# Filter work of the first pair in two tails, norm factors one token tile later, four gates ahead of the last branch

## The chip, the cores and the metric

The kernel runs on one core of a Trainium2 chip. The metric is the device time of one execution in microseconds (us); a comparison goes by the median of several executions.

## The reference

The input `x` has 512 tokens of width 1024, all float32. Two blocks of two layers each follow one another: two layers of the first kind (layer a), then two pairs of the second kind (layer b, cross attention, MLP).

```
def first_block(x, ...):                       # layer a, l = 0, 1
    h = rms_norm(x, norm_g[l]);  p = h @ w_in[l]
    y_a = short_conv_mixer(...); y_b = sparse_attention_mixer(...); y_c = pool_mixer(...)
    g = sigmoid(mgate)
    x = x + (g[0] * y_a + g[1] * y_b + g[2] * y_c) @ w_o[l]
...
def second_block(h, mem, ...):                 # pair i = 0, 1
    (aq, ak, av, hy, gq, gk, gv, go, glr, gates) = split_cols(rmsnorm(h) @ w_in[i])
    y_a = attention_mixer(aq, ak, av, ...) @ w_br_attn[i]
    spec = hyena_filter_spectra(z_pos, window, hy_w1[i], ...)   # depends on weights alone
    y_b = hyena_mixer(hy, hy_conv[i], spec, hy_skip[i]) @ w_br_hyena[i]
    y_c = gla_mixer(...) @ w_br_gla[i]
    h = h + (gate[0] * y_a + gate[1] * y_b + gate[2] * y_c) @ w_out[i]
    h = h + memory_cross_attention(...)
    h = h + square(relu(rmsnorm(h) @ mlp_w1[i])) @ mlp_w2[i]
```

In both attentions the heads of queries and keys are normalised: each head of 64 is multiplied by the reciprocal root of its mean square, and rotated by its position. `hyena_filter_spectra` sends a table of positions through a small network of two sine layers, forms four filters (two orders, two directions) under a window, and takes their Fourier transform.

## The kernel before, in words

Every float32 product is made of three matmuls of a rounded type, a high and a low part of each operand (`mm3`, lines 242 to 244). So each weight tile is loaded by an SP DMA into `wr`, its high part `wh` is made on ACT (line 220) and its low part `wl` on DVE (line 221), and the same split makes the high and low parts of every activation (`big`). `gemm_t` and `gemm_wide` are the two loops over such products: `gemm_t` makes 256 output columns at a time (a column chunk: 48 matmuls for 1024 rows of weights, 24 for 512), with the result transposed; `gemm_wide` makes 512 columns for four tiles of 128 tokens, each in a PSUM tile of its own, and then calls `evac(t, ps[t])` for the four tiles in turn.

The order of instructions on each engine is fixed when the program is built, from the order of the code and from priorities (`high_priority`); at run time each engine goes through its own list and waits where an operand is not there.

**Norm factors.** Queries and keys come out of `gemm_wide`. Its `evac` (`ev_qk`, lines 707 to 724 in layer a; `heads`, from line 1315, in layer b) copies the PSUM tile to SBUF on ACT (`lift`, line 326, a buffer of the pool s2), sums squares on DVE (`sums64`, line 578), and calls `rsqrt_small`: one small DVE instruction (line 583), then a power on POOL (line 584) over 4 to 8 columns, in the tile `sgk`. The next DVE instruction of that tile is the one that reads POOL's result (line 719 to `sig` in layer a, line 1327 in layer b); the rotation (lines 534 to 537) and the splits stand around it.

**Filters of a pair.** `filters(l)` sets up a generator, and `step_background` takes one step of it after every column chunk of `gemm_t`. For pair 0 that happens in the tail of the second layer a (26 chunks), for pair 1 in the first MLP (31 chunks). The steps are, in order: two sine layers (a matmul at line 1067, a chain of seven DVE instructions at lines 1069 to 1074, a sine on ACT at line 1075), the features `hA`, `hB` (lines 1081 to 1083), and then for each order `od` four steps that multiply features with taps (lines 1097, 1098) and with a window tile `win` that POOL's DMA queue loads into one buffer (line 1100), the sum of magnitudes (line 1108) that the matmul at line 1130 adds up, and eight transform steps.

**The last branch of layer b.** `finish_merge` calls `gate_out`, which for each pair of output tiles makes two gates (a column chunk of 48 matmuls on `h`), and multiplies them with a chunk of 24 matmuls on the branch's output `yb` (weights `w_br_hyena`). With `lead` 2 the gates of the first pair are made ahead. `yb` is what the second long convolution leaves: its last matmuls (`sd<-df,hy`), eight DVE instructions (lines 1290 to 1293), a product with `x2` from DRAM (line 1477) and a split.

Of the kernel before, what the change touches and what calls it, by code (L numbers as in the profile page):

```python
# [10 lines left out]
F32 = mybir.dt.float32  # L11
F32R = mybir.dt.float32r
# [7 lines left out]
P = 128  # L20
# [111 lines left out]
class Kernel:  # L132
    def __init__(self, ctx, tc, A, out, scratch=None):
        self.ctx, self.tc, self.A, self.out = ctx, tc, A, out
        self.nc = tc.nc
        pool = lambda name, **kw: ctx.enter_context(tc.tile_pool(name=name, **kw))
        self.cst = pool("cst", bufs=1)
        self.wp = pool("wp", bufs=3)
        self.bp = pool("bp", bufs=10)
        self.xp = pool("xp", bufs=9)  # L140
        self.sp = pool("sp", bufs=6)
        self.pp = pool("pp", bufs=6)
        self.dp = pool("dp", bufs=1, space=DRAM)
# [4 lines left out]
        self.background = None  # L148
        self.consts()

# [493 lines left out]
    def layer_a(self, l, st, next_norm, side=None):  # L644
# [62 lines left out]
        def qkv(c):  # L707
# [5 lines left out]
            def ev_qk(t, ps):  # L713
# [292 lines left out]

    def filters(self, l):

        nc, A = self.nc, self.A
        spec = self.dp.tile([2, 4, 3, P, 512], F32, tag=f"spec{l}", name=self.nm("spec"), bufs=1)  # L1010
        self.background, self.halves = self.filter_steps(l, spec), False
        next(self.background)
        return spec

    def filter_steps(self, l, spec):
        with self.tc.tile_pool(name=f"fg{l}", bufs=1, reuse_waits="tile") as fp:
            self.hp = fp
            yield from self.filter_body(l, spec, fp)

    def filter_body(self, l, spec, fp):  # L1020
# [3 lines left out]
        w12 = fp.tile([P, P], F32, tag="w12", name=self.nm("w12"))  # L1024
        cols = self.small(8, "hycol", bufs=1)
        nc.gpsimd.dma_start(w12[:33, 0:64], A["hy_w1_2"][l])
        nc.gpsimd.dma_start(w12[:64, 64:128], A["hy_w2_2"][l])
        for i, a in enumerate((A["hy_b1_2"][l], A["hy_b2_2"][l], A["hy_freq_2"][l, 0], A["hy_freq_2"][l, 1])):
            nc.gpsimd.dma_start(cols[:64, i : i + 1], a.rearrange("(p o) -> p o", o=1))
        zp = own("win")  # L1030
        nc.gpsimd.dma_start(zp[:33], A["c_zpos"])
        h1 = self.p2()
        h2 = self.p2()

# [28 lines left out]

        nxt = taps_w(0)
        for dst, lhs, rhs, i in ((h1, w12[:33, 0:64], zp[:33], 0), (h2, w12[:64, 64:128], h1[:64], 1)):
            ps = self.ps_sd()
            nc.tensor.matmul(ps[:64], lhs, rhs, start=True, stop=True)
            arg, n = self.p2()[:64], self.p2()[:64]
            nc.vector.tensor_scalar(arg, ps[:64], cols[:64, i : i + 1], cols[:64, 2 + i : 3 + i], ALU.add, ALU.mult)
            nc.vector.tensor_scalar(n, arg, 1.0 / (2 * math.pi), 12582912.0, ALU.mult, ALU.add)  # L1070
            nc.vector.tensor_scalar(n, n, 12582912.0, None, ALU.subtract)
            for part in (6.28125, 0.0019350051879882812, 3.0199159819567e-07):
                nc.vector.scalar_tensor_tensor(arg, n, -part, arg, ALU.mult, ALU.add)
            nc.vector.tensor_scalar(arg, arg, 3.1415925, -3.1415925, ALU.min, ALU.max)
            nc.scalar.activation(dst[:64], arg, AF.Sin)
            yield
        hB_ = hB.bitcast(F32)
        nc.gpsimd.memset(hB_[64:P], 0.0)
        nc.gpsimd.memset(hB_[64:65], 1.0)
        nc.gpsimd.memset(hB_[96:97], 1.0)  # L1080
        nc.vector.tensor_copy(hB[:64], h2[:64])
        nc.scalar.copy(hA[:64], h2[:64])
        nc.vector.tensor_tensor(hA[64:P], h2[:64], hA[:64].bitcast(F32), ALU.subtract)
        yield
        e = fp.tile([P, 4, 512], F32, tag="fe", name=self.nm("fe"))
        o = fp.tile([P, 4, 512], F32, tag="fo", name=self.nm("fo"))
        for od in range(2):
            w3 = nxt
# [45 lines left out]
            for m, (b, i) in enumerate(steps):  # L1134
# [19 lines left out]
                nc.gpsimd.dma_start(spec[od, b, i], f)  # L1154
                if m == 6 and od == 0:
                    nxt = taps_w(1)
# [138 lines left out]
    def layer_b(self, l, st, spec, next_norm):  # L1295
# [22 lines left out]
        def heads(c, t, ps, ng):  # L1318
# [6 lines left out]
            self.rsqrt_small(ss, ss, 1.0 / 64, n)  # L1325
            rs = rstd[:, t : t + 1]
            nc.vector.tensor_scalar(sigs[c][:, t * 4 : t * 4 + 4], ss[:, :4], rs, 0.125, ALU.mult, ALU.mult)
            v = lambda x: x.rearrange("p (g h d) -> p g h d", g=ng, h=2)
# [3 lines left out]
            self.split(qhl[c][:, t, :, 0], qhl[c][:, t, :, 1], r[:, :4])  # L1332
            if n > 4:
                nc.vector.tensor_scalar(ss[:, 4:6], ss[:, 4:6], rs, None, ALU.mult)
                nc.vector.tensor_tensor(r[:, 4:6], r[:, 4:6], ss[:, 4:6].unsqueeze(2).to_broadcast([P, 2, 64]), ALU.mult)
                self.split(kv[:, t, 0:2, 0], kv[:, t, 0:2, 1], r[:, 4:6])

        def ev_qkv(t, ps):
            ps = self.lift(ps)
            vs = ps[:, 384:512].rearrange("p (h d) -> p h d", h=2)  # L1340
            heads(0, t, ps, 3)
            self.split(kv[:, t, 2:4, 0], kv[:, t, 2:4, 1], vs, scale=rstd[:, t : t + 1])

        gv = self.big(F32)
# [3 lines left out]
        def ev_qg(t, ps):  # L1348
            nc.scalar.activation(gv[:, t, 0:256], ps[:, 256:512], AF.Copy, scale=rstd[:, t : t + 1])
            heads(1, t, self.lift(ps[:, 0:256]), 2)  # L1350

# [94 lines left out]
        with self.tc.tile_pool(name=f"gb{l}", bufs=16, reuse_waits="tile") as self.gp:  # L1446
            turn_lr()
            b, on = self.gla_begin(l, glr)
            self.gemm_t(W, 2304, 512, KD, h, ev_qk)
            self.background, self.halves = self.gla_steps(l, b, on, qk, gv), True  # L1450
            self.gate_out(W, 3872, h, A["w_br_attn_2"][l], ya, M, True, None)
# [12 lines left out]
        with self.tc.tile_pool(name=f"hb{l}", bufs=8, reuse_waits="tile") as self.hp:  # L1464
# [9 lines left out]
            for c in range(4):  # L1474
# [359 lines left out]
    def run(self, stop=None):  # L1834
# [3 lines left out]

        def fill(l):
            spec[l] = self.filters(l)  # L1840

# [49 lines left out]
```

## Time and profile before

| | |
|---|---|
| median of 3 runs | 3386.12 us (3383.73 to 3386.2) |
| profiled execution | 3385.05 us, span 3382.9 us |
| granted TensorE clock, mean | 0.997 |
| PE busy | 3309.0 us |
| DVE busy | 2335.5 us |
| ACT busy | 1509.5 us |
| POOL busy | 308.0 us |

Busy time is that in which the engine has an instruction under way. Matmuls overlap, so PE is counted busy while it works at any rate; how densely they follow is read from their starts or from their number in a window.

### The profile page before, as it was taken

How to read it: one execution, taken by the hardware profiler on the slowest of the kernel's cores; microseconds unless marked ns; L12 is line 12 of the kernel's file. 1: busy time of each engine (PE TensorE's matmuls, PEld its weight loads, DVE VectorE, ACT ScalarE, POOL GpSimd, SP SyncE). 2: the span in 40 equal slices, each digit the busy share in tenths (PEclk: the TensorE clock that was granted, in tenths of full speed). 3: DMA queues.
4: the chain of work that ended last, by engine and by line, in shares of the span. 5: the costliest groups of instructions: out<-in, count | busy, mean ns of one | idle time of the engine just before them, and what ended most of it. 6: DMA issues, size and time to landing. Idle time of an engine off the chain costs nothing. (4 is left out here: it accounts for less than half of the span.)

```text
span 3382.9 us, 42739 instructions
## 1 busy us (share of the span) xinstructions
PE 3309.0 (98%) x15768; PEld 2708.7 (80%) x15768; DVE 2335.5 (69%) x4405; ACT 1509.5 (45%) x2505; POOL 308.0 (9%) x480
## 2 busy tenths in 40 slices
PE   8999999999999999999999999999999999999999
PEld 6887888887777877788788888887778878888887
DVE  7976645976778778768666666867876876653354
ACT  6265433445644366533345443345663334533222
POOL 1001000011012110011011101101000101000000
PEclk9999999999999999999999999999999999999999
DMA  5322334332345423235452434433222545233332
GB/s 138 100 69 75 89 111 131 82 94 70 88 118 153 150 73 82 83 87 175 134 176 95 132 120 131 142 119 95 84 70 71 175 143 171 95 126 98 97 115 87
DMA packets 323537, 376.23 MB, mean 111 GB/s; under 512 B 23198, under 2 KB 281108, under 8 KB 323328
## 3 DMA queue, kind: packets, MB, share of 16 engines
q1 hardware_dynamic: 290944, 294.73, 29.1%
q0 software_dynamic: 32384, 78.78, 7.9%
q8 instruction: 124, 2.03, 0.3%
q14 instruction: 85, 0.70, 0.1%
HBM read 340.93 MB, written 32.51 MB: 110 GB/s over the span
## 5 line engine op out<-in xcount | busy, mean ns | idle before, releaser
L242 PE MATMUL mm<-big,wh 128*128 128x512 f32 (+1 forms) x3480 | 1367.9, 393 | 14.3 <-ACT big L220 6.8
L244 PE MATMUL mm<-big,wl 128*128 128x512 f32 (+1 forms) x3480 | 1363.9, 392 | 9.2 <-DVE wl L221 9.2
L243 PE MATMUL mm<-big,wh 128*128 128x512 f32 (+1 forms) x3480 | 1363.1, 392 | 0.4 <-DVE big L221 0.4
L220 ACT ACTIVATE wh<-wr 128x1024 fp32r<-128x1024 f32 (+1 forms) x528 | 551.1, 1044 | 752.7 <-PE mm L243 513.2
L221 DVE TENSOR_TENSOR wl<-wr,wh 128x1024 fp32r<-128x1024 f32 (+1 forms) x528 | 634.2, 1201 | 303.9 <-PE mm L244 202.9
L242 PEld LDWEIGHTS mm<-big,wh 128*128 128x128 f32 (+1 forms) x3480 | 654.2, 188 | 158.0 <-ACT big L220 8.3
L244 PEld LDWEIGHTS mm<-big,wl 128*128 128x128 f32 (+1 forms) x3480 | 654.5, 188 | 147.0 <-DVE wl L221 10.9
L243 PEld LDWEIGHTS mm<-big,wh 128*128 128x128 f32 (+1 forms) x3480 | 654.5, 188 | 136.4 <-DVE big L221 1.8
L242 PE MATMUL mm<-wh,big 128*128 128x512 f32 (+2 forms) x672 | 234.9, 350 | 5.0 <-ACT s L326 3.4
L243 PE MATMUL mm<-wl,big 128*128 128x512 f32 (+2 forms) x672 | 234.0, 348 | 5.6 <-DVE wl L221 5.6
L244 PE MATMUL mm<-wh,big 128*128 128x512 f32 (+2 forms) x672 | 232.2, 346 | 0.0
L220 ACT ACTIVATE big<-s 128x512 fp32r<-128x512 f32 (+1 forms) x196 | 103.6, 532 | 139.9 <-DVE s L537 64.6
L242 PEld LDWEIGHTS mm<-wh,big 128*128 128x128 f32 x672 | 126.8, 189 | 23.5 <-ACT s L326 5.7
L243 PEld LDWEIGHTS mm<-wl,big 128*128 128x128 f32 x672 | 126.9, 189 | 22.3 <-DVE wl L221 8.2
L244 PEld LDWEIGHTS mm<-wh,big 128*128 128x128 f32 x672 | 126.7, 189 | 14.8
L221 DVE TENSOR_TENSOR big<-s,big 128x512 fp32r<-128x512 f32 (+1 forms) x196 | 109.0, 566 | 18.8 <-ACT big L220 17.2
L1801 DVE TENSOR_TENSOR s<-s 128x512 f32<-128x512 f32 x64 | 43.6, 687 | 99.9 <-ACT s L1800 99.9
L220 ACT ACTIVATE pt<-sd 128x512 fp32r<-128x512 f32 (+3 forms) x160 | 76.9, 489 | 68.9 <-PE sd L349 50.5
L221 DVE TENSOR_TENSOR pt<-sd,pt 128x512 fp32r<-128x512 f32 (+3 forms) x160 | 87.8, 551 | 28.2 <-ACT pt L220 26.2
L955 DVE TENSOR_TENSOR x<-mm,x 128x512 f32<-128x512 f32 x48 | 33.0, 687 | 75.0 <-PE mm L244 75.0
L349 PE MATMUL sd<-c,p 128*128 128x128 f32 x480 | 80.9, 277 | 3.3 <-DVE sm L616 1.2
L349 PEld LDWEIGHTS sd<-c,p 128*128 128x128 f32 x480 | 55.2, 140 | 33.5 <-issue 11.4
(424 smaller groups left out, 3998.8 us busy)
## 6 DMA issues: line engine op xcount, KB each, us to landing
wr<-in_w_in_dram SPq DMA_DIRECT2D x208, 512.0 KB, 3.7
wr<-in_mlp_w_dram SPq DMA_DIRECT2D x128, 512.0 KB, 3.5
wr<-in_w_in_dram SPq DMA_DIRECT2D x72, 256.0 KB, 2.9
res<-x POOLq DMA_DIRECT2D x64, 256.0 KB, 3.1
x<-res POOLq DMA_DIRECT2D x48, 256.0 KB, 3.0
F<-spec SPq DMA_DIRECT2D x36, 256.0 KB, 3.8
wr<-in_w_o_dram SPq DMA_DIRECT2D x16, 512.0 KB, 3.4
wt<-in_c_dftf_dram POOLq DMA_DIRECT2D x32, 256.0 KB, 4.2
```

Source lines behind the costliest of these rows:

```text
L220: nc.scalar.activation(H, src, AF.Copy)
L221: nc.vector.tensor_tensor(L, src, H.bitcast(F32), ALU.subtract)
L242: mm(out, aH, bH, start=first, stop=False, **kw)
L243: mm(out, aH, bL, start=False, stop=False, **kw)
L244: mm(out, aL, bH, start=False, stop=last, **kw)
L349: self.nc.tensor.transpose(dst_ps[: s.shape[-1], i * P : i * P + s.shape[0]], s, self.ident)
L955: self.nc.vector.tensor_tensor(X, ps, X, ALU.add)
L1801: nc.vector.tensor_tensor(a, a, a, ALU.mult)
```

## The change

Three edits.

**Norm factors.** `gemm_wide` takes from each `evac` a function and calls it after the next tile's `evac`. What reads POOL's result (`sig`, the scaling of the keys, the split of the keys) goes into that function, `norms`; the rotation and the split of the queries stay. `lift` takes its buffers from the pool p2 (also of 128x512 tiles, used by the attention and the filters) and no more from s2.

**Filters.** `filters` gets a list of orders and a pace: of 12 chunks, `pace` take a step. Pair 0's sine layers and order 0 go into the tail of the first layer a (pace 8), its order 1 into the tail of the second (pace 7), where the features are loaded again from DRAM; pair 1 stays in the first MLP at pace 11.

**Gates.** `lead` of layer b's last branch is 4 and no more 2.

```diff
     def gemm_wide(self, segs, stat, evac, ntok=NT):
...
+            rest = None
             for t in range(ntok):
-                evac(t, ps[t])
+                after = evac(t, ps[t])
+                if rest is not None:
+                    rest()
+                rest = after
+            if rest is not None:
+                rest()

     def lift(self, ps):
-        c = self.s2()[:, : ps.shape[1]]
+        c = self.p2()[:, : ps.shape[1]]
...
         if self.background is not None and (whole or self.halves):
+            self.chunks += 1
+            if self.chunks * self.pace // 12 == (self.chunks - 1) * self.pace // 12:
+                return
...
                 self.rsqrt_small(ss, ss, 1.0 / 64, 8)
-                nc.vector.tensor_scalar(sigv[:, t], ss[:, 0:4], 0.125, None, ALU.mult)
                 r = self.s2().rearrange("p (g h d) -> p g h d", g=2, h=4)
                 self.rope(r, src, [tb[:, t] for tb in tabs_qk], 0, 4)
-                nc.vector.tensor_tensor(r[:, 1], r[:, 1], ss[:, 4:8].unsqueeze(2).to_broadcast([P, 4, 64]), ALU.mult)
-                for i in range(2):
-                    self.split(hls[i][:, t, :, 0], hls[i][:, t, :, 1], r[:, i])
+                self.split(hls[0][:, t, :, 0], hls[0][:, t, :, 1], r[:, 0])
+
+                def norms():
+                    nc.vector.tensor_scalar(sigv[:, t], ss[:, 0:4], 0.125, None, ALU.mult)
+                    nc.vector.tensor_tensor(r[:, 1], r[:, 1], ss[:, 4:8].unsqueeze(2).to_broadcast([P, 4, 64]), ALU.mult)
+                    self.split(hls[1][:, t, :, 0], hls[1][:, t, :, 1], r[:, 1])
+
+                return norms
...
+            if len(ods) == 1:
+                for i, t in enumerate((hA, hB)):
+                    nc.gpsimd.dma_start(self.feats[i], t)
+        else:
+            for i, t in enumerate((hA, hB)):
+                nc.gpsimd.dma_start(t, self.feats[i])
+            yield
...
-        for od in range(2):
+        for od in ods:
...
         return self.finish_merge(W, 3872 + D, h, A["w_br_hyena_2"][l], yb, M, A["w_out_2"][l], next_norm,
-                                 lambda: self.cross_mem(l), 2)
+                                 lambda: self.cross_mem(l), 4)
...
-        st = self.layer_a(0, st, A["norm_g"][1])
+        st = self.layer_a(0, st, A["norm_g"][1], lambda: fill(0, (0,), 8))
+        self.finish_background()
...
-        st = self.layer_a(1, st, A["ln_mix_2"][0], lambda: fill(0))
+        st = self.layer_a(1, st, A["ln_mix_2"][0], lambda: fill(0, (1,), 7))
...
-            st = self.mlp(l, st, *((A["ln_mix_2"][1], lambda: fill(1)) if l == 0 else (None,)))
+            st = self.mlp(l, st, *((A["ln_mix_2"][1], lambda: fill(1, (0, 1), 11)) if l == 0 else (None,)))
```

Layer b's `heads` is changed in the same way as `ev_qk`. Lines below number the kernel that they stand in; behind line 150 the changed kernel's numbers are larger by 1 to 35.

The order on DVE in layer a's second wide product, before: the end of the third token tile and the fourth (`sgk_2655` is the fourth tile's, `wl_2777` the low part of the fourth weight tile of the product that follows).

```order
L537 TENSOR_TENSOR s_475_2642<-s_475_2642,s_476_2643 128x512
L578 TENSOR_REDUCE sgk_2655<-s_479_2656 128x8
L722 TENSOR_TENSOR s_475_2642<-s_475_2642,sgk_2635 128x256
L221 TENSOR_TENSOR big_2275<-s_475_2642,big_2275 128x4x64
L583 TENSOR_SCALAR sgk_2655<-sgk_2655 128x8
L534 TENSOR_TENSOR s_481_2663<-s_477_2653,rt_559 128x8x32
L221 TENSOR_TENSOR big_2276<-s_475_2642,big_2276 128x4x64
L719 TENSOR_SCALAR sig_2278<-sgk_2655 128x4
L536 TENSOR_TENSOR s_480_2662<-s_477_2653,rt_558 128x512
L221 TENSOR_TENSOR wl_2777<-wr_2775,wh_2776 128x1024
```

The same place in the changed kernel (`sgk_2651` is the fourth tile's).

```order
L589 TENSOR_REDUCE sgk_2651<-s_479_2652 128x8
L545 TENSOR_TENSOR s_481_2658<-p_477_2649,rt_559 128x8x32
L594 TENSOR_SCALAR sgk_2651<-sgk_2651 128x8
L547 TENSOR_TENSOR s_480_2657<-p_477_2649,rt_558 128x512
L735 TENSOR_SCALAR sig_2278<-sgk_2631 128x4
L736 TENSOR_TENSOR s_475_2637<-s_475_2637,sgk_2631 128x256
L222 TENSOR_TENSOR wl_2777<-wr_2775,wh_2776 128x1024
L548 TENSOR_TENSOR s_480_2657<-s_480_2657,s_481_2658 128x512
L222 TENSOR_TENSOR big_2276<-s_475_2637,big_2276 128x4x64
L735 TENSOR_SCALAR sig_2278<-sgk_2651 128x4
```

Before, two instructions stand between the one that sends a tile to POOL (`sgk<-sgk`, line 583) and the one that reads what comes back (`sig<-sgk`); now there are six, a weight split among them, and that split stands ahead of the last reader.

The order on PE where the last branch of pair 0 begins, before: the end of the second long convolution (`sd<-df,hy`) and the first product on `yb` (`big_14160`, `big_14161`).

```order
L244 MATMUL sd_14143<-df_14071,hy_14114 128x256
L242 MATMUL sd_14143<-df_14071,hy_14122 128x256
L243 MATMUL sd_14143<-df_14073,hy_14122 128x256
L244 MATMUL sd_14143<-df_14071,hy_14123 128x256
L242 MATMUL mm_14727<-big_14160,wh_14730 128x512
L243 MATMUL mm_14727<-big_14161,wh_14730 128x512
```

The same place in the changed kernel: the end of the convolution, the gates' product on `h` (`mm_14740`, `mm_14741`), of which the first two and the last two rows stand here, and the first product on `yb` (`big_14173`, `big_14174`).

```order
L243 MATMUL sd_14156<-df_14084,hy_14135 128x256
L244 MATMUL sd_14156<-df_14086,hy_14135 128x256
L245 MATMUL sd_14156<-df_14084,hy_14136 128x256
L244 MATMUL mm_14740<-big_10042,wh_14743 128x512
L245 MATMUL mm_14740<-big_10040,wl_14744 128x512
...
L244 MATMUL mm_14741<-big_10043,wh_14773 128x512
L245 MATMUL mm_14741<-big_10041,wl_14774 128x512
L243 MATMUL mm_14806<-big_14173,wh_14809 128x512
L244 MATMUL mm_14806<-big_14174,wh_14809 128x512
```

Between the last matmul of the convolution and the first on `yb` there were none and are now 41; seven more of the gates' matmuls stand between the convolution's own. In the rest of the branch the last three products on `yb`, of 24 matmuls each, now follow one another with no gates between.

How many matmuls of the tail's own products stand on PE between two steps of pair 0's filters:

| from, to | before | now |
|---|---|---|
| first sine layer (L1067), second | 73 | 53 |
| second sine layer, first features product (L1097) | 43 | 38 |
| order 0: last features product, sum of magnitudes (L1130) | 70 | 96 |
| order 1: the same | 72 | 144 |

On POOL's DMA queue two stores and two loads of 256 KB are new (the features); all other instructions are the same in number on every engine.

## Rows read from the trace of the kernel before

**Rows 1.** The page, busy time of each engine (us, share of the span, instructions).

```profile
PE 3309.0 (98%) x15768; PEld 2708.7 (80%) x15768; DVE 2335.5 (69%) x4405; ACT 1509.5 (45%) x2505; POOL 308.0 (9%) x480
```

**Rows 2.** What PE waited for over the whole span: total us, times, longest us.

```profile
PE mm L244 <- DVE wl L221: 9.2, 4, 2.7
PE mm L242 <- ACT big L220: 6.8, 3, 3.3
...
PE sd L1130 <- DVE p L1108: 3.1, 1, 3.1
PE sd L242 <- ACT hy L220: 2.7, 3, 1.2
...
PE sd L1097 <- DVE hA L1083: 1.3, 1, 1.3
```

**Rows 3.** Windows: length, busy us of each engine, PEclk, DMA share, GB/s.

```profile
400.00:600.00 200.00, 200.00 (x961) 167.42 (x960) 103.94 (x151) 71.66 (x101) 9.14 (x16) 1.00 0.40 118
978.10:981.50 3.40, 3.40 (x8) 2.00 (x7) 3.40 (x7) 1.29 (x3) 0.00 (x0) 0.50 0.48 154
1198.00:1244.00 46.00, 40.06 (x215) 33.91 (x215) 37.57 (x111) 28.41 (x61) 8.52 (x7) 1.00 0.32 81
1647.00:1650.50 3.50, 3.50 (x10) 2.50 (x8) 1.29 (x2) 0.56 (x1) 0.00 (x0) 0.52 0.57 203
1650.60:1655.60 5.00, 5.00 (x23) 4.14 (x23) 3.50 (x5) 1.68 (x2) 0.00 (x0) 1.00 0.00 0
```

**Rows 4.** Timeline of PE: start, us, what, idle before and what ended it.

```profile
290.15 0.50 PE L244 MATMUL mm<-big,wl 128*128 128x512 f32 x1 [2.69 <-DVE wl L221]
...
977.78 1.78 PE L1130 MATMUL sd<-p,c 128*128 128x512 f32 x2 [3.07 <-DVE p L1108]
...
1645.70 0.50 PE L242 MATMUL mm<-big,wh 128*128 128x512 f32 x1 [3.25 <-ACT big L220]
1646.43 0.50 PE L243 MATMUL mm<-big,wh 128*128 128x512 f32 x1 [0.22 <-DVE big L221]
```

**Rows 5.** What PE waited for from 1198 to 1260 us.

```profile
PE mm L243 <- DVE wl L221: 2.1, 3, 1.3
PE sd L1378 <- ACT t L548: 1.7, 1, 1.7
PE mm L242 <- ACT s L326: 1.6, 2, 1.3
PE mm L242 <- DVE ld L1357: 1.0, 1, 1.0
```

**Rows 6.** What DVE waited for over the whole span.

```profile
DVE sig L719 <- POOL sgk L584: 18.4, 12, 1.6
...
DVE sig L1327 <- POOL sgk L584: 15.9, 16, 1.2
...
DVE p L1100 <- DMA win<-in_c_window_dram: 4.7, 2, 2.9
```

**Rows 7.** Timeline of DVE in the first layer a and before pair 0's last branch.

```profile
179.48 1.22 DVE L221 TENSOR_TENSOR wl<-wr,wh 128x1024 fp32r<-128x1024 f32 x1
...
181.09 0.17 DVE L719 TENSOR_SCALAR sig<-sgk 128x4 f32<-128x4 f32 x1
...
279.55 1.22 DVE L221 TENSOR_TENSOR wl<-wr,wh 128x1024 fp32r<-128x1024 f32 x1
...
288.20 0.17 DVE L719 TENSOR_SCALAR sig<-sgk 128x4 f32<-128x4 f32 x1 [1.53 <-POOL sgk L584]
...
288.88 1.22 DVE L221 TENSOR_TENSOR wl<-wr,wh 128x1024 fp32r<-128x1024 f32 x1
...
1649.21 1.34 DVE L1477 TENSOR_TENSOR ld<-big,ld 128x512 f32<-128x512 f32 x2 [2.23 <-DMA ld<-x2s]
```

**Rows 8.** Timeline of POOL, two of its powers.

```profile
179.38 1.68 POOL L584 TENSOR_TENSOR sgk<-sgk,c 128x8 f32<-128x8 f32 x1 [3.47 <-DVE sgk L583]
...
279.78 2.81 POOL L584 TENSOR_TENSOR sgk<-sgk,c 128x8 f32<-128x8 f32 x1 [3.22 <-DVE sgk L583]
```

More of the change, by code (lines that the diff above doesn't have):

```diff
@@ L148, in __init__ @@
         self.background = None
+        self.pace, self.chunks = 12, 0
         self.consts()
@@ L1004, in index, with filters, filter_steps, filter_body @@
         return out
[L1007 to L1011, printed above, removed]
+    def filters(self, l, ods, pace):
+        if 0 in ods:
+            self.spec = self.dp.tile([2, 4, 3, P, 512], F32, tag=f"spec{l}", name=self.nm("spec"), bufs=1)
+            self.feats = self.dp.tile([2, P, 512], F32R, tag=f"feats{l}", name=self.nm("feats"), bufs=1)
+        self.background, self.halves = self.filter_steps(l, self.spec, ods), False
+        self.pace, self.chunks = pace, 0
         next(self.background)
-        return spec
-    def filter_steps(self, l, spec):
-        with self.tc.tile_pool(name=f"fg{l}", bufs=1, reuse_waits="tile") as fp:
+        return self.spec
+    def filter_steps(self, l, spec, ods):
+        with self.tc.tile_pool(name=f"fg{l}{ods[0]}", bufs=1, reuse_waits="tile") as fp:
             self.hp = fp
-            yield from self.filter_body(l, spec, fp)
-    def filter_body(self, l, spec, fp):
+            yield from self.filter_body(l, spec, fp, ods)
+    def filter_body(self, l, spec, fp, ods):
         nc, A = self.nc, self.A
         own = lambda tag, bufs=1: fp.tile([P, 512], F32, tag=tag, name=self.nm(tag), bufs=bufs)
[L1024 to L1033, printed above, removed]
         hA = fp.tile([P, 512], F32R, tag="hA", name=self.nm("hA"))
@@ L1062, in table @@
             return [x.rearrange("p (i z f) -> p i z f", i=2, z=2) for x in t]
[L1064 to L1075, printed above, removed]
-            yield
@@ L1077, in filter_body @@
[L1077 to L1084, printed above, removed]
+        nxt = taps_w(ods[0])
+        if ods[0] == 0:
+            w12 = fp.tile([P, P], F32, tag="w12", name=self.nm("w12"))
+            cols = self.small(8, "hycol", bufs=1)
+            nc.gpsimd.dma_start(w12[:33, 0:64], A["hy_w1_2"][l])
+            nc.gpsimd.dma_start(w12[:64, 64:128], A["hy_w2_2"][l])
+            for i, a in enumerate((A["hy_b1_2"][l], A["hy_b2_2"][l], A["hy_freq_2"][l, 0], A["hy_freq_2"][l, 1])):
+                nc.gpsimd.dma_start(cols[:64, i : i + 1], a.rearrange("(p o) -> p o", o=1))
+            zp = own("win")
+            nc.gpsimd.dma_start(zp[:33], A["c_zpos"])
+            h1 = self.p2()
+            h2 = self.p2()
+            for dst, lhs, rhs, i in ((h1, w12[:33, 0:64], zp[:33], 0), (h2, w12[:64, 64:128], h1[:64], 1)):
+                ps = self.ps_sd()
+                nc.tensor.matmul(ps[:64], lhs, rhs, start=True, stop=True)
+                arg, n = self.p2()[:64], self.p2()[:64]
+                nc.vector.tensor_scalar(arg, ps[:64], cols[:64, i : i + 1], cols[:64, 2 + i : 3 + i], ALU.add, ALU.mult)
+                nc.vector.tensor_scalar(n, arg, 1.0 / (2 * math.pi), 12582912.0, ALU.mult, ALU.add)
+                nc.vector.tensor_scalar(n, n, 12582912.0, None, ALU.subtract)
+                for part in (6.28125, 0.0019350051879882812, 3.0199159819567e-07):
+                    nc.vector.scalar_tensor_tensor(arg, n, -part, arg, ALU.mult, ALU.add)
+                nc.vector.tensor_scalar(arg, arg, 3.1415925, -3.1415925, ALU.min, ALU.max)
+                nc.scalar.activation(dst[:64], arg, AF.Sin)
+                yield
+            hB_ = hB.bitcast(F32)
+            nc.gpsimd.memset(hB_[64:P], 0.0)
+            nc.gpsimd.memset(hB_[64:65], 1.0)
+            nc.gpsimd.memset(hB_[96:97], 1.0)
+            nc.vector.tensor_copy(hB[:64], h2[:64])
+            nc.scalar.copy(hA[:64], h2[:64])
+            nc.vector.tensor_tensor(hA[64:P], h2[:64], hA[:64].bitcast(F32), ALU.subtract)
+            yield
+            if len(ods) == 1:
[4 more added lines that the diff above has]
+                nc.gpsimd.dma_start(t, self.feats[i])
+            yield
@@ L1154, in filter_body @@
                 nc.gpsimd.dma_start(spec[od, b, i], f)
-                if m == 6 and od == 0:
+                if m == 6 and od != ods[-1]:
                     nxt = taps_w(1)
@@ L1325, in heads @@
             self.rsqrt_small(ss, ss, 1.0 / 64, n)
-            rs = rstd[:, t : t + 1]
-            nc.vector.tensor_scalar(sigs[c][:, t * 4 : t * 4 + 4], ss[:, :4], rs, 0.125, ALU.mult, ALU.mult)
             v = lambda x: x.rearrange("p (g h d) -> p g h d", g=ng, h=2)
@@ L1332, in heads, with norms @@
             self.split(qhl[c][:, t, :, 0], qhl[c][:, t, :, 1], r[:, :4])
[L1333 to L1336, printed above, removed]
+            def norms():
+                rs = rstd[:, t : t + 1]
+                nc.vector.tensor_scalar(sigs[c][:, t * 4 : t * 4 + 4], ss[:, :4], rs, 0.125, ALU.mult, ALU.mult)
+                if n > 4:
+                    nc.vector.tensor_scalar(ss[:, 4:6], ss[:, 4:6], rs, None, ALU.mult)
+                    nc.vector.tensor_tensor(r[:, 4:6], r[:, 4:6], ss[:, 4:6].unsqueeze(2).to_broadcast([P, 2, 64]), ALU.mult)
+                    self.split(kv[:, t, 0:2, 0], kv[:, t, 0:2, 1], r[:, 4:6])
+            return norms
         def ev_qkv(t, ps):
@@ L1340, in ev_qkv @@
             vs = ps[:, 384:512].rearrange("p (h d) -> p h d", h=2)
-            heads(0, t, ps, 3)
+            norms = heads(0, t, ps, 3)
             self.split(kv[:, t, 2:4, 0], kv[:, t, 2:4, 1], vs, scale=rstd[:, t : t + 1])
+            return norms
         gv = self.big(F32)
@@ L1349, in ev_qg @@
             nc.scalar.activation(gv[:, t, 0:256], ps[:, 256:512], AF.Copy, scale=rstd[:, t : t + 1])
-            heads(1, t, self.lift(ps[:, 0:256]), 2)
+            return heads(1, t, self.lift(ps[:, 0:256]), 2)
         def ev_gl(t, ps):
@@ L1449, in layer_b @@
             self.gemm_t(W, 2304, 512, KD, h, ev_qk)
-            self.background, self.halves = self.gla_steps(l, b, on, qk, gv), True
+            self.background, self.halves, self.pace = self.gla_steps(l, b, on, qk, gv), True, 12
             self.gate_out(W, 3872, h, A["w_br_attn_2"][l], ya, M, True, None)
@@ L1837, in run, with fill @@
         spec = [None, None]
-        def fill(l):
-            spec[l] = self.filters(l)
+        def fill(l, ods, pace):
+            spec[l] = self.filters(l, ods, pace)
         st = self.norm_begin(A["norm_g"][0])
```

## The prediction

> **What bounds the kernel now.** I read the busy times first: PE 3309.0 us of a span of 3382.9, DVE at 69%, ACT and POOL far below [rows 1]. So PE is the bound, and the only time to win is that in which PE waits or runs at a lower rate. A count of matmuls tells the rate: 23 start in 5.00 us at a granted clock of 1.00, 0.22 us each [rows 3]. I then read the list of what PE waited for, and found five entries in places that the change touches [rows 2]: the wait for a weight's low part (9.2 us in four waits, the longest 2.7), for `big` from ACT (6.8 in three, the longest 3.3), for `hy` from ACT (2.7 in three, the longest 1.2), for the filter's magnitudes at L1130 (3.1) and for the features `hA` (1.3). The timeline places them: 290.15 in layer a's second wide product, 977.78 in the second layer a's tail, 1645.70 at pair 0's last branch [rows 4].
>
> Two of these stalls have a tail that no list of waits shows. From 978.1 to 981.5 the granted clock is 0.50, from 1647.0 to 1650.5 it is 0.52, the lower of the two levels (1.2 of 2.4 GHz), and then 1.00 again [rows 3]. Both stretches begin right after a wait of more than 3 us [rows 4]. So such a stall costs its wait and about (1 - 0.52) x 3.5 = 1.7 us more. The wait of 2.69 us at 290.15 is not among them.
>
> The start of layer b is the widest patch: from 1198 to 1244 PE is busy 40.06 of 46.00 us, and DVE 37.57 [rows 3]. PE waits four ways there, 2.1 + 1.7 + 1.6 + 1.0 = 6.4 us up to 1260 [rows 5]. All come from DVE and ACT being late with that product's results, and DVE in turn loses 15.9 us in 16 waits for POOL's power, so 8.0 in each of the two layers [rows 6].
>
> **Gates ahead of the last branch.** Before, PE goes from the convolution straight to `yb`. It waits 1.2 us for `hy` inside the convolution [rows 2], then 3.25 and 0.22 us for `yb` [rows 4], then runs 3.5 us at 0.52 [rows 3]: 1.2 + 3.25 + 0.22 + 1.7 = 6.4 us. The change puts seven gate matmuls in the first gap (7 x 0.22 = 1.5 us against 1.2) and 41 behind the convolution (41 x 0.22 = 9.0 us against 3.25). `yb`'s second half comes later: its `x2` waits 2.23 us for a DMA and its product starts at 1649.21 [rows 7], 3.5 us behind PE's first matmul on `yb`. With 9.0 us of cover instead of 3.25 that half is done about where it is wanted, after half of the first 24 matmuls. The gates are made anyway, so the added cost is nothing in matmuls. What it takes away is cover at the end: three products on `yb` follow each other, each of 24 x 0.22 = 5.3 us, for which DVE has a weight split of 1.22 [rows 7] and six passes of 1.34 / 2 = 0.67 [rows 7], 5.2 us together. That is even, so 0 to 1 us may come back per layer. I take the full 6.4 off, less 0.2: 6.2 x 2 = **-12.4**. The bounds are 4.7 (the clock falls elsewhere) and 6.4 per layer.
>
> **Norm factors, layer a.** The wait that PE feels is the last weight split, which starts at 288.88, right behind a wait of 1.53 us for POOL [rows 7]; PE stands 2.69 us for it [rows 4]. This is the 2.7 of the list, once per layer. DVE lost 18.4 us in 12 such waits, 1.5 each [rows 6]. Now six instructions instead of two stand between a tile's way to POOL and its way back, a weight split of 1.22 among them, and the split that PE wants has moved ahead of the last reader. Three earlier waits of 1.5 in the same product are 4.5 us, more than the 2.69 needed, so the split should be there in time: 2.7 x 2 = **-5.4**. If only half of the waits went, 2.2 of the 2.69 would still go; if none, 0.
>
> **Norm factors, layer b.** At most the 6.4 us of rows 5 can go per layer. DVE would need 37.57 us for its work where PE needs 40.06, so DVE is barely the faster of the two, and a chain that goes from PE to ACT to DVE and back won't be seamless. I take 5.5 of 6.4: **-11.0** for two. The bounds are 2.5 (only the weight-split waits and a little) and 6.4 per layer. `lift` from p2: the same copy from another pool, at nothing, as long as a buffer is free; see the rivals.
>
> *The port.* The move only helps if DVE's other work runs while POOL's power does. Two cases in the trace show it. POOL's power began at 179.38 and lasted 1.68 us [rows 8], DVE began a weight split 0.10 us later, which took its usual 1.22, and the reader at 181.09 waited for nothing [rows 7]. In the other order, the split began at 279.55, POOL's power at 279.78, and the power lasted 2.81 us [rows 8]: it waited some 1.1 us for DVE. So DVE does not lose time to POOL here, POOL does to DVE, and six instructions on DVE (1.22 and five shorter) are about as long as 2.81.
>
> The Trainium skill ("SBUF — State Buffer", section "Who interferes with whom") says that a DVE instruction with two SBUF inputs and a GpSimd instruction that reads SBUF share a port, and that whichever issues second is fully blocked until the first has finished. The power of 2.81 us agrees; the split at 179.48, which was second, does not. By the rule each power would hold DVE as long as its own wait did, the two layer terms would be nil, and the sum would be that of the first rival.
>
> **Filters.** Gone are the wait of 3.07 us at 977.78 [rows 4] and the low clock behind it, 3.4 x 0.50 = 1.7 [rows 3]: 4.8 us. It came from the DMA of the one window buffer, for which DVE waited 2.9 us and 4.7 in all [rows 6], with only 70 matmuls (15.4 us) between the last features product and L1130; with 96 (21.1 us) or 144 the chain has 5.7 us more room, more than the 3.07 and the rest. In the first layer a's tail there is room for the steps themselves: from 400 to 600 DVE is busy 103.94 of 200 us, and PE all of it [rows 3]. The price is in the sine layers: 53 matmuls instead of 73 between the two, 4.4 us less cover, and 38 instead of 43 up to the features, 1.1 us less, where PE already waited 1.3 [rows 2]. The second makes the wait 2.4. The first has no wait of its own in the rows that I show; its cover shrinks in a tail where DVE has less to do, so I take 0.4 of a possible 4.4. Together +1.1 + 0.4 = 1.5, and the term is -4.8 + 1.5 = **-3.3**, with bounds of -4.8 and +2.4 (4.4 + 1.1 and the 1.7 of a fallen clock). Pair 1 at pace 11: the list shows one wait each at L1130 and L1097 [rows 2], both pair 0's, so there is nothing to gain or lose, 0. The four feature DMAs stand on POOL's queue well ahead of their use: 0, or at worst a wait like the window's 2.9.
>
> **Sum.** -12.4 - 5.4 - 11.0 - 3.3 = -32.1, against the profiled execution's 3385.05: 3353. That execution is 1.07 us under the median of 3386.12, which is inside what runs differ by. What a measurement can tell from no change is about 0.2%, 6.8 us.
>
> **The rivals.**
> *POOL's port blocks DVE after all.* Then every power that is overlapped stops DVE as it did before, and gates and filters remain: 3385.05 - 12.4 - 3.3 = 3369. For it: in 12 of 16 cases in layer a and all 16 in layer b DVE stood still until POOL was done [rows 6]. Against: the case at 179.48. Chance 0.10.
> *DVE bounds layer b, and the sine layers stall.* Layer b gives 2.5 each, the filters cost 2.4: 3385.05 - 12.4 - 5.4 - 5.0 + 2.4 = 3365. For it: 37.57 against 40.06. Against: DVE's work from 1198 to 1244 is not all wanted there by PE. Chance 0.20.
> *The lifts wait for p2, and it is slower.* A lift frees a PSUM tile; if it is late PE waits, as it does 1.6 us in two waits now [rows 5]. p2 is also taken by softmax tiles and by filters, which hold theirs through DMA waits. There are 32 lifts in the four layers. To lose the 32.1 us and 6.8 more, each would have to hold PE 39 / 32 = 1.2 us, a little more than the one long wait of 1.3 [rows 5]: 3392. Against: in each product only the first one or two lifts meet other users of the pool. Chance 0.05 for 1.2 us or more each.
> *The same.* Lifts that wait half as much, 0.6 us, or a clock that falls four or five times more, along with the port: about 3381. Chance 0.06.
>
> **How the numbers follow.** The forecast has 0.59 and its own range is 3346 to 3361, from the bounds of its terms. With the second rival (3365) and most of the first (3369) the range is 3345 to 3371, which leaves out 0.11 above and some 0.08 below and at the edge. Faster by over 0.2%, so under 3379.3: 0.59 + 0.10 + 0.20 = 0.89. Same 0.06, slower 0.05.
>
> **What would show it.** Right: no wait of PE for `big` from ACT at the last branches, and PEclk 9 or more there; no readers of `sgk` among DVE's large waits (15.9 and 18.4 us), with powers that last up to 2.8 us; PE's wait of 2.7 at the weight split gone in both layers a; PE busy 44 of 46 us at layer b's start; no wait at L1130, and one of 2 to 3 us at L1097 in the first layer a's tail. Wrong: weight splits on DVE of over 1.22 us under a power (the port); ACT's lifts waiting for a DVE reader of p2; a low clock in the first tail; a new wait of PE for DVE in the last three products on `yb`.

## The result and the profile after

The changed kernel takes 3344.28 us (median of 4 runs, 3343.23 to 3346.32) against 3384.97 us, 40.7 us less; the ratio is 0.9881, 95% interval 0.9863 to 0.9898. The forecast was 3353, from 3345 to 3371: the direction and the three places are right, the gain is 8.6 us larger, and the time lies 0.7 us below the range. The profiled execution took 3346.32 us, with a span of 3344.4.

The busy times of the changed kernel:

```profile
PE 3297.5 (99%) x15768; PEld 2707.5 (81%) x15768; DVE 2331.6 (70%) x4405; ACT 1510.0 (45%) x2505; POOL 324.2 (10%) x484
```

PE and DVE do what they did. PE's idle time, span less busy time, falls from 73.9 to 46.9 us; that is 27.0 of the 38.5 us by which the span shrank, and the other 11.5 are PE's busy time, with the same number of matmuls. What PE waits for now, over the whole span (the answer to [rows 2]):

```profile
PE sd L360 <- DMA big<-in_x_dram: 6.5, 2, 6.0
PE sd L1409 <- ACT t L559: 3.6, 2, 1.8
...
PE mm L245 <- DVE wl L222: 2.6, 2, 1.9
...
PE mm L243 <- ACT gl L1466: 1.4, 1, 1.4
...
PE sd L1123 <- DVE hA L1102: 1.2, 1, 1.2
...
PE mm L243 <- ACT big L221: 0.3, 1, 0.3
```

The 9.2 us for the weights' low part are 2.6, the 6.8 for `big` are 0.3, and the waits for `hy` and at the magnitudes have left the list. The wait for `hA` is 1.2 us, not the 2.4 that I had priced. New is one of 1.4 us for ACT at the linear attention. Of DVE's waits for POOL's powers at L719 and L1327 [rows 6] none is left in its list.

Three windows of the changed kernel, to set beside [rows 3]: the first layer a's tail with order 0's filters in it, layer b's start, and the stretch of pair 0's last branch.

```profile
400.00:600.00 200.00, 200.00 (x893) 163.62 (x893) 136.22 (x196) 78.25 (x108) 20.49 (x37) 1.00 0.44 131
1182.00:1228.00 46.00, 44.15 (x241) 38.29 (x240) 39.94 (x121) 30.00 (x64) 10.84 (x7) 1.00 0.33 89
1600.00:1650.00 50.00, 49.89 (x240) 41.34 (x239) 32.27 (x52) 16.82 (x24) 2.89 (x5) 1.00 0.45 137
```

PE is busy all through the first tail although DVE does 136.22 us there instead of 103.94; at layer b's start it is busy 44.15 of 46 us instead of 40.06; the last branch has neither wait nor low clock.

For the sum I compare starts of the same PE instructions, one at the end of each stretch. These are ten of the kernel before:

```profile
306.16 0.49 PE L555 MATMUL sd<-c,big 128*128 128x128 f32 x3
577.26 0.47 PE L384 MATMUL sd<-c,nsq 128*128 128x1 f32 x3
855.65 0.38 PE L555 MATMUL sd<-c,big 128*128 128x128 f32 x2
1178.45 0.39 PE L384 MATMUL sd<-c,nsq 128*128 128x1 f32 x3
1244.16 0.50 PE L1378 MATMUL sd<-t,t 128*128 128x512 f32 x1 [1.69 <-ACT t L548]
1418.05 0.37 PE L1571 MATMUL sd<-gl,gl 64*128 64x128 f32 x1
1691.56 0.49 PE L349 MATMUL sd<-c,mt 128*128 128x128 f32 x3
2365.52 0.50 PE L1378 MATMUL sd<-t,t 128*128 128x512 f32 x1 [1.67 <-ACT t L548]
2537.82 0.37 PE L1571 MATMUL sd<-gl,gl 64*128 64x128 f32 x1
2811.29 0.38 PE L349 MATMUL sd<-c,mt 128*128 128x128 f32 x2
```

The same ten of the changed kernel:

```profile
304.54 0.38 PE L566 MATMUL sd<-c,big 128*128 128x128 f32 x2
596.20 0.37 PE L395 MATMUL sd<-c,nsq 128*128 128x1 f32 x2
871.72 0.38 PE L566 MATMUL sd<-c,big 128*128 128x128 f32 x2
1165.34 0.39 PE L395 MATMUL sd<-c,nsq 128*128 128x1 f32 x3
1223.94 0.50 PE L1409 MATMUL sd<-t,t 128*128 128x512 f32 x1 [1.85 <-ACT t L559]
1394.41 0.37 PE L1602 MATMUL sd<-gl,gl 64*128 64x128 f32 x1
1661.60 0.44 PE L360 MATMUL sd<-c,mt 128*128 128x128 f32 x2 [0.56 <-DVE mt L1677]
2328.90 0.50 PE L1409 MATMUL sd<-t,t 128*128 128x512 f32 x1 [1.76 <-ACT t L559]
2506.09 0.37 PE L1602 MATMUL sd<-gl,gl 64*128 64x128 f32 x1
2772.86 0.44 PE L360 MATMUL sd<-c,mt 128*128 128x128 f32 x2 [0.57 <-DVE mt L1677]
```

| stretch up to | end before | end after | change in the stretch |
|---|---|---|---|
| first layer a's second wide product | 306.16 | 304.54 | -1.6 |
| end of the first layer a (order 0 added) | 577.26 | 596.20 | +20.6 |
| second layer a's second wide product | 855.65 | 871.72 | -2.9 |
| end of the second layer a (sine layers and order 0 gone) | 1178.45 | 1165.34 | -29.2 |
| layer b 0, wide products | 1244.16 | 1223.94 | -7.1 |
| layer b 0, begin of the linear attention | 1418.05 | 1394.41 | -3.4 |
| layer b 0, last branch | 1691.56 | 1661.60 | -6.3 |
| cross, MLP, layer b 1, wide products | 2365.52 | 2328.90 | -6.7 |
| layer b 1, begin of the linear attention | 2537.82 | 2506.09 | +4.9 |
| layer b 1, last branch | 2811.29 | 2772.86 | -6.7 |
| end | 3382.9 | 3344.4 | -0.1 |

So the filters gave 20.6 - 29.2 = -8.6 us, the gates -13.0, layer b's wide products -13.8, layer a's -4.5 (the start of the program took 1.4 us longer in this execution, so nearly -3 each), and the linear attention +1.5, with opposite signs in the two layers.

### The profile page after: what moved, and what is told of

The parts are those of the page before. It is cut to its first block, busy times and chain, and to the rows that moved or that the text cites. A ratio compares the mean times of both kernels' runs of the same rounds, so it can differ in the third digit from the quotient of the medians.

```text
span 3344.4 us, 42721 instructions
## 1 busy us (share of the span) xinstructions
PE 3297.5 (99%) x15768; PEld 2707.5 (81%) x15768; DVE 2331.6 (70%) x4405; ACT 1510.0 (45%) x2505; POOL 324.2 (10%) x484
## 4 chain that ended last, share of the span: by engine, by line
PE 85%; DVE 8%; ACT 5%; issue 1%; DMA 1%; POOL 0%; SPq 0%; DVEq 0%; ACTq 0%; POOLq 0%
PE mm L243 24%; PE mm L244 24%; PE mm L245 24%; PE sd L360 2%; PE sd L243 2%; PE sd L244 2%; PE sd L245 2%; DVE wl L222 2%; PE sd L647 2%; ACT t L576 1%; DVE idx L1016 1%; DVE m L1015 1%; ACT wh L221 1%; ACT p L626 1%; PE sd L1637 0%
## 5 line engine op out<-in xcount | busy, mean ns | idle before, releaser
L221 ACT ACTIVATE big<-s 128x512 fp32r<-128x512 f32 (+2 forms) x196 | 103.8, 534 | 102.8 <-DVE s L1832 40.0
L222 DVE TENSOR_TENSOR big<-s,big 128x512 fp32r<-128x512 f32 (+2 forms) x196 | 109.1, 565 | 19.1 <-ACT big L221 17.1
L595 POOL TENSOR_TENSOR sgk<-sgk,c 128x8 f32<-128x8 f32 (+2 forms) x32 | 65.1, 2033 | 258.4 <-DVE sgk L594 241.3
```

The lines of the kernel that those rows point to most:

```text
L221: nc.scalar.activation(H, src, AF.Copy)
L222: nc.vector.tensor_tensor(L, src, H.bitcast(F32), ALU.subtract)
L595: nc.gpsimd.tensor_tensor(dst, dst, self.mhalf[:, :n], ALU.pow)
```

## The experiments

Each comparison names the median and, in brackets, the lowest and highest run; the kernel before had 3384.4 to 3385.4 beside them.

**One edit at a time.** Kernels that hold the filters' edit, the norm factors' edit, or

```diff
-                                 lambda: self.cross_mem(l), 2)
+                                 lambda: self.cross_mem(l), 4)
```

alone.

> The kernel before with the filters' edit alone. Theory (each edit works in its own stretch and the parts add up): the stretch from the first layer a's tail to the end of the second one's is 8.6 us shorter in the changed kernel, the first MLP 0.6 us longer, so about 8 us faster than before (ratio 0.9976). Rival (the tails gain because the norm factors had already put DVE ahead when they begin): the edit alone gives no more than the 3.3 us of the prediction.

Measured: 3377.8 us (3373.32 to 3386.01), ratio 0.998 (0.997 to 0.9989): 6.6 us faster. The theory holds, with a part less: by the starts of the same instructions the tails give 8.6 us, and 1.9 are given back in the second layer a's wide product, where the wait of 2.7 us, which is still there, was followed by a low clock in this execution.

> The kernel before with the norm factors' edit alone, lifts in p2 included. Theory (parts add up): 2.9 to 3.0 us less in each layer a, 7.1 to 7.2 us less in each of layer b's first products, together 20 us; what the begin of the linear attention makes of it in the two layers b (3.4 us less, 4.9 us more in the changed kernel) comes with this edit, so 18.5 to 20 us faster (ratio 0.9943). Rival (POOL's port blocks DVE): near 0. Second rival (the shift at the linear attention comes from the filters or the gates): 20 us faster and both layers b alike from there on.

Measured: 3370.97 us (3370.21 to 3373.34), ratio 0.9961 (0.9949 to 0.9973): 13.5 us, so both the port's rival and the sum of 18.5 to 20 are wrong. The products do give what they give in the changed kernel (3.0 and 3.0 in layers a, 7.1 and 7.2 in layers b), but 2.9 and 3.0 us are lost at the begin of the linear attention, in both layers alike.

> The kernel before with lead 4 alone. Theory: 6.2 and 6.7 us less at the two last branches, so 12.9 us faster (ratio 0.9962), no low clock at 1647 and 2767 us. Rival (part of that gain belongs to DVE's earlier work through the other edits): less than 10 us.

Measured: 3370.81 us (3368.03 to 3372.26), ratio 0.9961 (0.9947 to 0.9974): 13.6 us. The two stretches are 6.2 and 6.8 us shorter, on their own; the theory holds.

The three sum to 33.7 us, and the changed kernel gives 40.7. The spans of the profiled executions differ by less: 6.9 + 12.7 + 17.0 = 36.6 us for the three edits, 38.5 for all together. The stretch that the sum misses most is the linear attention of layer b 0, with -1.1, +2.9 and -1.6 us for one edit each and -3.4 for all; part of that is a low clock that the kernel before shows there and the changed kernel does not. Where the rest of the 7 us lies is not settled.

**The pool of the lifts.** In the first of these kernels the norm factors' edit is alone, in the second all three edits are in:

```diff
-        c = self.p2()[:, : ps.shape[1]]
+        c = self.s2()[:, : ps.shape[1]]
```

> The norm factors' edit alone with the lifts still in s2. Theory (the later reading of POOL's result does it, the pool does not matter): the same 18.5 to 20 us as with p2. Rival (s2's buffers are now held a tile longer, so the lifts wait for them): less than half of that, with waits of ACT's lifts for DVE's readers. Second rival (p2 is what makes the second layer b's linear attention late, by 4.9 us): some 5 us faster than with p2.

Measured: 3365.93 us (3363.39 to 3367.13), ratio 0.9943 (0.9931 to 0.9956): 18.5 us, 5 more than with p2. Theory and second rival hold together: the deferral gives the gain, and with this edit alone p2 is worse than s2. The wait of PE for ACT at the linear attention, 1.4 us in each layer with p2, is gone. In the list of the edit with p2 it stands as

```profile
PE mm L242 <- ACT gl L1451: 2.8, 2, 1.4
```

> The changed kernel with the lifts back in s2. Theory (p2 costs 3 us at the linear attention of each layer b where norm factors alone are changed, and 5 at the second layer b of the changed kernel): 3 to 5 us faster than the changed kernel, so 3339 to 3341. Rival (the first layer b's gain there came with p2): the first layer b loses what the second gains, and the time stays at 3344.

Measured: 3348.2 us (3345.62 to 3348.77), ratio 0.9889 (0.9875 to 0.9902): 4 us slower than with p2, where the theory said 3 to 5 faster. The intervals of the two ratios overlap, so slower is not sure, but 3 to 5 faster is ruled out. The rival is nearer: layer b 1 gains 3.3 us at the linear attention and layer b 0 loses 3.9 there, with the same wait of 1.4 us for ACT now in layer b 0, and a low clock behind the wait at L1409 in each layer. So the stall is in one layer with one pool and in the other with the other. The pool alone does not decide that: the filters' edit alone, with its lifts in s2, has the same wait of 1.40 us in layer b 0 (at 1376.43), and the kernel before, with s2 too, has it nowhere. The pool has no worth of its own that holds in both kernels.

**The trip to POOL.** In the kernel before, with readers where they were:

```diff
         nc.vector.tensor_scalar(dst, src, mul, 1e-6, ALU.mult, ALU.add)
+        if heads:
+            nc.vector.tensor_scalar(dst, dst, 0.0, 0.05, ALU.mult, ALU.add)
+            return
         nc.gpsimd.tensor_tensor(dst, dst, self.mhalf[:, :n], ALU.pow)
```

> The kernel before with the trip to POOL taken out: in the heads' norm factors a DVE instruction writes a constant where POOL's power wrote the factor, so the normalisation is left out; all readers stay where they were. Theory (what the norm factors' edit gives is the time of those trips): as fast as that edit with lifts in s2, 18.5 us less than before, within 3. Rival (the edit gives more or less than the trips, by the order that it changes): off by more than 3 us, above all at layer b's start, where the deferral takes 6.7 us per layer.

Measured: 3364.01 us (3363.08 to 3366.67), ratio 0.9936 (0.9923 to 0.995): 20.8 us, 2.3 more than the deferral with lifts in s2. So the deferral gets 18.5 of the 20.8 us that the trips cost. By the starts of the same instructions the four wide products with queries and keys gain 19.4 us with the deferral and 19.7 without the trips, nearly the same. What PE still waits for at layer b 0's start, without the trips and then with the deferral:

```profile
PE sd L1381 <- ACT t L548: 1.9, 1, 1.9
```

```profile
PE sd L1394 <- ACT t L555: 2.0, 1, 2.0
```

One wait of the four of [rows 5] stays, in either way, so it isn't POOL's.

**The filters' window and pace.** First the kernel before with a second window buffer:

```diff
-        w12 = fp.tile([P, P], F32, tag="w12", name=self.nm("w12"))
+        w12 = fp.tile([P, 4, 512], F32, tag="fe", name=self.nm("w12"))[:, 0, :P]
...
-                win = own("win")
+                win = own("win", 2)
```

> The kernel before with two window buffers in the filters (the first sine layer's weights move into a buffer that is used later, to make room). Theory (the one window buffer makes DVE late for the magnitudes at L1130, as the prediction said): the wait of 3.07 us there and the low clock that can follow are gone, 3 to 5 us faster. Rival (DVE is late because all 27 steps lie in one tail, one in each chunk): the wait at L1130 stays within 1 us of what it was, and the time within 0.1%.

Measured: 3378.86 us (3376.24 to 3380.67), ratio 0.9981 (0.9973 to 0.999): 6.0 us, the theory, and a little over its size. One buffer more gives almost what the whole filters' edit gives. The wait at L1130 is now

```profile
PE sd L1130 <- DVE p L1108: 0.3, 1, 0.3
```

Then the filters' edit with `fill(0, (0,), 12)`, `fill(0, (1,), 12)` and `fill(1, (0, 1), 12)`.

> The filters' edit alone with pace 12 for all three: pair 0 still in two tails, but a step in every chunk until they are done. Theory (pace decides, more matmuls between two steps): the wait at L1130 comes back in one or both tails and at least half of the 6.6 us that the edit gives is lost. Rival (parting the work over two tails is enough): within 2 us of the edit at its own paces, 3376 to 3380.

Measured: 3389.95 us (3384.85 to 3393.52), ratio 1.0011 (1.0003 to 1.002): slower than before, 12 us slower than with its own paces. The theory holds and more than half is lost. The stall has come back in both tails, 3.40 and 1.89 us long in the timeline of PE (the next expectation has 2.1 for the second):

```profile
430.73 0.70 PE L1145 MATMUL sd<-p,c 128*128 128x512 f32 x1 [3.40 <-DVE p L1123]
...
988.00 1.12 PE L1145 MATMUL sd<-p,c 128*128 128x512 f32 x2 [1.89 <-DVE p L1123]
```

and DVE waits for the window in each, by its list over the whole span:

```profile
DVE p L1115 <- DMA win<-in_c_window_dram: 8.5, 4, 2.6
```

Then both, pace 12 and two window buffers.

> The filters' edit alone at pace 12 (which was 5 us slower than before) with two window buffers. Theory (pace matters only because the one window buffer's DMA must fit between two steps): the waits at L1130 of 3.4 and 2.1 us are gone and it is about as fast as the edit at its own paces, 3376 to 3380. Rival (at pace 12 the DVE work itself is too dense): waits of over 1.5 us remain there and it stays above 3384.

Measured: 3381.4 us (3378.27 to 3384.36), ratio 0.9992 (0.9982 to 1.0001): 8.6 us of the 12 come back, and the wait is

```profile
PE sd L1145 <- DVE p L1123: 0.2, 1, 0.2
```

The mechanism is the theory's; the time is 1.4 us above its bound, in a kernel whose profiled execution shows six low clocks before the last microseconds, against four with its own paces. Of the 3.6 us that it takes more than with those, the starts place 1.4 and 1.6 in the two tails. PE's idle time in each tail is the same within 0.3 us, so they are no new wait but starts that follow less closely in many places. Why they do is not settled, and the rival (DVE's work too dense) is not excluded for this part.

**What is left.** The changed kernel with the linear attention's weights in another pool (`wl = self.s2()` for `wl = self.p2()` in `gla_begin`), the same with two window buffers, and the changed kernel with pair 1 at pace 12.

> The changed kernel with the linear attention's small weights loaded into a buffer of s2 instead of p2. Theory (in the second layer b these six small DMAs wait for a buffer of p2, which the lifts and the filters now take too, and land after DVE needs them): the wait of DVE of 4.4 us and PE's of 1.4 us there are gone, 2 to 5 us faster than the changed kernel, 3339 to 3342. Rival (the DMAs wait for something else on POOL's queue): no change, 3343 to 3346.

Measured: 3342.5 us (3341.4 to 3343.78), ratio 0.9874 (0.9857 to 0.989). The wait of 1.4 us for ACT is gone, as the theory says, and the gain is 1.8, less than it said. The wait for a weight split behind DVE's scans in the same layer stays; it was 1.94 us in the changed kernel, and here it is 1.64:

```profile
2497.39 0.50 PE L245 MATMUL mm<-big,wl 128*128 128x512 f32 x1 [1.64 <-DVE wl L222]
```

> The same with two window buffers in the filters as well. Theory (with steps this far apart the one window buffer costs nothing any more): within 1 us of the kernel without the second buffer. Rival (the window still holds DVE up in the tails): 2 us or more faster.

Measured: 3343.43 us (3341.83 to 3344.98), within 1 us of the kernel without the second buffer. At these paces the one window buffer costs nothing that these runs can tell.

> The changed kernel with pair 1's filters at pace 12, as before. Theory (in the MLP there was no wait to win, and the 0.6 us longer there are the pace's): within 1 us of the changed kernel. Rival (pace 11 saves a wait that the list of before did not show): 2 us or more slower.

Measured: 3343.8 us (3343.04 to 3344.18), 0.5 us from the changed kernel. Pair 1's pace is worth nothing. The first of the three is the fastest kernel of all, but its interval overlaps with that of the changed one.

## Why the prediction was right or wrong

**Gates: right.** Forecast -12.4, measured -13.0 in the changed kernel and 13.6 us alone. No matmul on `yb` waits. `yb`'s second half does come late, its DMA of `x2` was again waited for (two rows of DVE's timeline):

```profile
1625.34 0.69 DVE L1508 TENSOR_TENSOR ld<-big,ld 128x512 f32<-128x512 f32 x1 [0.96 <-DMA ld<-x2s]
...
1630.23 0.69 DVE L1508 TENSOR_TENSOR ld<-big,ld 128x512 f32<-128x512 f32 x1 [1.02 <-DMA ld<-x2s]
```

The last product starts at 1630.23, 12 us behind the convolution's end at about 1618.4; the gates and the first half of `yb`'s own matmuls covered it. The three products in a row cost nothing that shows.

**Norm factors, layer a: right**, -2.9 us in the second layer a against -2.7, and 3.0 in each where the edit stands alone.

**Norm factors, layer b: the term was mis-sized.** I took 5.5 and set 6.4 as a bound, from the list of waits; the products gave 7.1 and 7.2 us. The bound also held 1.7 us at L1378 that were not POOL's and stayed, so the waits that went are 4.7 us of the list. A list of waits counts idle time from the modelled end of a matmul, and not what a wait costs between two starts. One of the waits before, in layer b 0:

```profile
1202.22 0.39 PE L242 MATMUL mm<-wh,big 128*128 128x512 f32 x1
1203.95 0.50 PE L243 MATMUL mm<-wl,big 128*128 128x512 f32 x1 [1.34 <-DVE wl L221]
```

The list has 1.34 us; the starts are 1.73 apart where 0.23 is usual, 1.50 more, and the next matmul follows after 0.33, 0.10 more. That is 1.6 us for a wait of 1.34. What the six waits cost beyond this was not taken apart.

**The linear attention: left out altogether**, -3.4 and +4.9 us. [rows 2] had a sign of it: of its four waits for a weight's low part only two, of 2.69 us, stand in the layers a; the other two stand here, one in each layer b. In the kernel before (a row of PE's timeline, then the window behind it):

```profile
1411.22 0.50 PE L244 MATMUL mm<-big,wl 128*128 128x512 f32 x1 [1.92 <-DVE wl L221]
...
1411.60:1415.00 3.40, 3.40 (x10) 2.63 (x9) 2.91 (x10) 2.23 (x5) 0.00 (x0) 0.50 0.50 154
...
2532.61 0.50 PE L244 MATMUL mm<-big,wl 128*128 128x512 f32 x1 [1.93 <-DVE wl L221]
...
2532.60:2536.00 3.40, 3.39 (x15) 2.82 (x16) 2.91 (x10) 1.84 (x5) 0.00 (x0) 1.00 0.46 154
```

In the changed kernel it is layer b 1 where the clock falls:

```profile
2499.26 0.50 PE L245 MATMUL mm<-big,wl 128*128 128x512 f32 x1 [1.94 <-DVE wl L222]
...
2499.80:2503.20 3.40, 3.40 (x9) 2.65 (x8) 2.91 (x10) 2.39 (x6) 0.00 (x0) 0.50 0.50 154
```

So 1.7 us of either figure is a low clock, in layer b 0 before and in layer b 1 after. Beside that, this wait is 0.67 us in layer b 0 of the changed kernel, and the wait of 1.40 us for `gl` is new in layer b 1. There it was a matter of the buffer of the small weights, since it went when they were loaded into another pool. What decides in which layer it happens is not settled; the pool is only part of it.

**Filters: the step that failed.** "Together +1.1 + 0.4 = 1.5, and the term is -4.8 + 1.5 = -3.3, with bounds of -4.8 and +2.4." Measured: -8.6 by stretches. The cause was right: the one window buffer (6.0 us by a second buffer alone, and the same stall back at pace 12). Both sizes were off. The price did not come: the wait for `hA` is 1.2 us with 38 matmuls of cover, as it was 1.3 with 43, since DVE's chain for it is about as much shorter: before, a weight split of 1.23 us at 940.15 stood between its first two instructions (939.21 and 941.30), and in the changed kernel they follow each other (387.94 and 388.77). The first sine layer does not wait with 53. And the stall cost more than its wait and its clock: matmul by matmul, the second buffer alone takes 6.5 us off this tail, 5.6 of them from the stall on, instead of 4.8. The other 1.0 lies ahead of the filters' first matmul, in a wait that I had not looked at: before, while POOL filled two tiles of the filters, a DVE instruction of the attention took 1.18 us, and PE waited for it.

```profile
910.35 0.55 POOL L1050 MEMSET wt<- 64x512 f32 x1
910.81 0.55 POOL L1078 MEMSET hB<- 64x512 f32 x1
...
910.46 1.18 DVE L617 TENSOR_SCALAR p<-p,sm 128x512 f32<-128x512 f32 x1
...
911.79 0.63 PE L349 MATMUL sd<-c,p 128*128 128x128 f32 x4 [0.79 <-DVE p L617]
```

It takes 1.18 us or a little more in all five profiles with the filters' order of before, and 0.49 with two window buffers, where the memsets come later; in the changed kernel the wait is gone too. No run moved the memsets alone. If the filters' edit wins the same at both places, that is 6.6 of the 8.6; the other 2 us were not taken apart.

**The rivals.** POOL's powers do not hold DVE up; they last longer themselves. The third token tile in the second wide product of the changed kernel's first layer a, in the timelines of POOL and then DVE:

```profile
277.18 4.37 POOL L595 TENSOR_TENSOR sgk<-sgk,c 128x8 f32<-128x8 f32 x1 [1.61 <-DVE sgk L594]
```

```profile
278.22 1.21 DVE L222 TENSOR_TENSOR wl<-wr,wh 128x1024 fp32r<-128x1024 f32 x1
...
282.99 0.18 DVE L735 TENSOR_SCALAR sig<-sgk 128x4 f32<-128x4 f32 x1
```

The power lasts 4.37 us, to 281.55, more than the 2.81 that I had taken as its longest [rows 8]. The weight split under it takes 1.21, as ever; none of the 512 of this size lasts over 1.23 us in either kernel. The reader comes at 282.99 and waits for nothing, because the change left it more room than the six instructions that I counted. Of the rule of the Trainium skill ("SBUF — State Buffer", section "Who interferes with whom") these powers bear out that POOL can be made to wait by DVE, and not that DVE waits where POOL's power began first. That is said of powers alone: beside the memsets above DVE did take longer, 1.18 us instead of 0.49. Lifts that wait for p2 and the sine layers' stall did not come either.

**The range** was too narrow below: my own bounds of gain sum to 35.8 us, and the span shrank by 38.5. They lead to 3349 at the lowest, so the 3346 that I gave as coming from them does not follow.

## What to carry to other kernels

Put a short trip to a slow engine one tile ahead of its reader: that got 18.5 of the 20.8 us that the trips cost here. Where work in the background waits for a load into one buffer, a second buffer and a wider pace buy the same thing; try the buffer first, since three changed lines gave 6.0 of the 6.6 us. Price a stall on the bound engine above its idle time: here 5.6 us came of cutting a wait from 3.07 to 0.3, with the low clock behind it. And look at what the background work makes other engines do before its first step: two memsets on POOL lay over a DVE instruction that PE was waiting for, and some 1.0 us went there.

## What the runs showed of the hardware

The low clock behind a wait is no fixed price. The plainest case is in the kernel before itself: of the two waits of 1.92 and 1.93 us at the linear attention, shown above, the clock fell behind the first and stayed at 1.00 behind the second. Behind the wait of 2.69 us at 290.15 the clock of the kernel before stayed at 1.00; with pace 12 it fell at the same wait, of 2.70 us, which ended at 292.20:

```profile
291.60:295.00 3.40, 2.80 (x7) 2.22 (x8) 3.28 (x7) 1.78 (x3) 0.00 (x0) 0.51 0.70 218
```

With the gates' edit alone, whose filters are those of before, the wait at L1130 was 2.22 us instead of 3.07, and no low clock followed:

```profile
977.43 1.12 PE L1130 MATMUL sd<-p,c 128*128 128x512 f32 x2 [2.22 <-DVE p L1108]
```

```profile
978.60:982.00 3.40, 3.40 (x16) 2.67 (x15) 3.24 (x6) 2.14 (x4) 0.00 (x0) 1.00 0.36 121
```

So part of the differences between these kernels, about 1.7 us at a time, is whether a clock fell, and differences below 3 us are not told apart by one profile each.
